# The head of an encoder kernel: x loaded by tokens, its squares summed along rows, and half of the bucket marks made on ScalarE

## The chip, the cores and the metric

One core of a Trainium2 chip runs the whole program in one launch. The time of a run is the device time of that core in microseconds (us). A profile of one execution stands beside the timed runs; its span goes from the first to the last instruction. The engines are named as in the profile: PE is TensorE (PEld its weight loads), DVE is VectorE, ACT is ScalarE, POOL is GpSimd, SP is SyncE, which here issues every load and store.

## What is computed

A trunk of two layers on one sequence of 256 tokens and 2048 features, in float32. Only what the head of the program touches matters here:

```python
cond = jax.nn.silu(c)
for l in range(DEPTH):
    mod = cond @ w_ada[l] + b_ada[l]
    sh_a, sc_a, g_a, sh_m, sc_m, g_m = jnp.split(mod, 6, axis=-1)
    h = _rmsnorm(x) * (1.0 + sc_a) + sh_a        # x / sqrt(mean(x*x) + eps), per token
    proj = h @ w_in[l]
    ...                                          # two kinds of attention, output projection
    # the first kind adds to its scores
    rel = positions[:, None, :] - pi[:, :, None]
    bias = bias_table[_t5_bucket(rel)]           # 32 buckets of relative distance
    ...
    x = x + g_a * mix
    ...                                          # adaLN again, squared-ReLU MLP of width 8192
return _rmsnorm(x, final_norm_g)
```

Of the 32 buckets, 16 are for keys ahead of the query and 16 for the others. In each half the buckets 0 to 7 hold a single distance each (0 to 7), the buckets 8 to 15 hold ranges of distances. One bucket, number 16 (ahead, at distance 0), never occurs.

## The kernel before

Activations are kept feature-major: `self.x` is 128 partitions (features of one k tile) by 16 k tiles by 256 tokens. Weights come from memory in f32; most are split into a rounded part and a rest (`weights`: `hi` made on ACT, `lo` on DVE) and go through PE in three products. The first six blocks of layer 0 are not split: `by_k` multiplies them whole (its line with `whole[k]`, L240).

Buffers come from pools that go round: five 8 KB buffers with tag `raw` for adaLN weights and unsplit weights, four each with tags `hi` and `lo` of 4 KB, six with tag `t` for short-lived activations, 40 with tag `u`, eight PSUM banks. A tile waits until the earlier holder of its buffer is done with. A scheduler writes the order of the instructions of each engine when the program is built; each engine then runs its own list strictly in order, and SP issues the loads in the order of its list.

The head runs in this order.

- `setup` loads `c`, the vectors, constants (`K`) and positions, and then x, already turned by the host (`xT`), as four loads of 512 KB. PE spreads `c` over all partitions (four products with a row of ones, `pc`), and ACT makes `cond` with Silu. `bias_setup` prepares positions and the bucket table on DVE and ACT.
- `sumsq` squares x on ACT, two k tiles at a time (eight squares of 128x512), and DVE adds the results up (seven adds). Then `rstd` lets PE sum over partitions (`pn`, four small products of 128x1 for the two token halves), ACT takes the square root, DVE the reciprocal, and PE spreads the result over the partitions with `ident`.
- `first_norm_then_by_k` takes the 16 k tiles in eight blocks p of two. For each block: DVE multiplies x by the norm (`ht`), four adaLN sums give the block's shift and scale (`ada_sums`: a pass of DVE over a 128x2048 weight tile against `cond`, twice for the shift and twice for the scale, and small adds that end in `mod`), ACT applies them (`hf`) and rounds (`h`), DVE makes the rest of the rounding, and PE multiplies by 24 weight tiles of `w_a` into six open PSUM banks.
- Into the first four blocks another piece is threaded (`FILL`): `bias_marks` and `bias_part` for a quarter of the bias table each. `bias_marks` makes eight marks, for four buckets each: ACT squares the distance to the bucket's centre (`sq`, 128x512), DVE compares it with the bucket's squared half width and writes ones and zeros (`oh`). `bias_part` multiplies the marks by the bucket table on PE (`pb`, 16 products), and ACT copies the result into `self.bias` at the next block.

The loads of a block are issued in this order: its four adaLN tiles (1 MB each), then its four weight tiles (384 KB each). An adaLN tile needs a free `raw` buffer, so its issue waits for the sum on DVE that has used up an older one, and the weight loads stand behind it in SP's list.

Of the kernel before, what the change touches and what calls it, by code (L numbers as in the profile page):

```python
# [9 lines left out]
F32 = mybir.dt.float32  # L10
F32R = mybir.dt.float32r
I32 = mybir.dt.int32
AF = mybir.ActivationFunctionType
ALU = mybir.AluOpType
AX = mybir.AxisListType

P = 128
T = 256
D = 2048
NK = D // P  # L20
# [22 lines left out]
C_W2 = 168  # L43
C_FREQ = 176
C_SGN = 177
NCONST = 178

V_BADA = 0
V_SUBLN = 192
# [20 lines left out]
def consts():  # L70
    c = np.zeros((P, NCONST), np.float32)
    p = np.arange(P)
    c[p, C_DELTA + p % 32] = 1.0
    c[p, C_PERM + (p ^ 32)] = 1.0
    for g in range(8):
        for r in range(4):
            b = 4 * g + r
            n = b % 16
            lo, hi = BUCKET_FROM[n], BUCKET_FROM[n + 1] - 1
            sign = -1.0 if b < 16 else 1.0  # L80
            rows = slice(32 * r, 32 * r + 32)
            if b == 16:
                c[rows, C_CB + g], c[rows, C_W2 + g] = 0.0, -1.0
            else:
                c[rows, C_CB + g] = -sign * (lo + hi) / 2.0
                c[rows, C_W2 + g] = ((hi - lo) / 2.0 + 0.25) ** 2
    c[:, C_FREQ] = np.asarray(INV_FREQ, np.float32)[p % 32]
    c[:, C_SGN] = np.where(p % 64 < 32, -1.0, 1.0)
    return c
# [10 lines left out]
class Trunk:  # L100
# [230 lines left out]
    def setup(self):  # L331
        nc, io, cp = self.nc, self.io, self.cp
        self.ada_plan()
        self.cond = cp.tile([P, D], F32, name="cond")
        row = self.wp.tile([1, D], F32, tag="raw", name="c_row", bufs=5)
        nc.sync.dma_start(row, io["c"])
        self.vec = cp.tile([P, NVEC], F32, name="vec")
        nc.sync.dma_start(self.vec, io["vec"])
        self.eps = cp.tile([P, 1], F32, name="eps")
        nc.gpsimd.memset(self.eps, EPS)  # L340
        self.K = cp.tile([P, NCONST], F32, name="K")
        nc.sync.dma_start(self.K, io["consts"])
        self.pos = cp.tile([P, T + 8], I32, name="pos")
        nc.sync.dma_start(self.pos, io["pos"])
        self.ones = cp.tile([P, P], F32, name="ones")
        nc.gpsimd.memset(self.ones, 1.0)
        self.bias_setup()
        self.rel = [self.bias_rel(0)]
        for j in range(4):
            c = slice(512 * j, 512 * j + 512)  # L350
            ps = self.bank("pc").rearrange("p a b -> p (a b)")
            nc.tensor.matmul(ps, self.ones[:1], row[:, c], start=True, stop=True)
            nc.scalar.activation(self.cond[:, c], ps, AF.Silu)
        self.ident = cp.tile([P, P], F32, name="ident")
        make_identity(nc, self.ident)
        self.x = cp.tile([P, NK, T], F32, name="x")
        for q in range(4):
            nc.sync.dma_start(self.x[:, 4 * q : 4 * q + 4], io["xT"][:, 4 * q : 4 * q + 4])
        acc = None
        for k in range(0, NK, 2):  # L360
            acc = self.sumsq(acc, self.x[:, k : k + 2])
        return acc

    def fills(self):
        m = {"l": self.lambdas, "r": self.rope_setup}
# [61 lines left out]
    def bias_marks(self, a):  # L427

        nc, K = self.nc, self.K
        half = lambda s, dt=F32: self.up.tile([P, 2 * T], dt, tag="u", name=self.name(s))  # L430
        r = self.rel.pop(0) if self.rel else self.bias_rel(a)
        self.marks = []
        for g in range(8):
            sq = self.t("sq")
            nc.scalar.activation(sq, r, AF.Square, bias=K[:, C_CB + g : C_CB + g + 1])
            oh = half("oh", F32R)
            nc.vector.tensor_scalar(oh, sq.rearrange("p a b -> p (a b)"), K[:, C_W2 + g : C_W2 + g + 1], None, ALU.is_le)
            self.marks.append(oh)

    def bias_part(self, a):  # L440
# [61 lines left out]
    def rstd(self, acc, n, warm=False):  # L502

        nc = self.nc
        bank = self.bank("pn")
        ps, r = bank[:, 0, :2], self.s("rms")
        acc = acc[:2] + acc[3:]
        if warm:
            self.warm(acc[-2], 8)
        for i, a in enumerate(acc):  # L510
            for t in range(2):
                nc.tensor.matmul(
                    ps[:, t : t + 1], a[:, t * P : (t + 1) * P], self.ones[:, :1],
                    start=i == 0 and t == 0, stop=i == len(acc) - 1 and t == 1, skip_group_check=True,
                )
        if warm:
            self.warm(acc[-1], 6)
        nc.scalar.activation(r, ps, AF.Sqrt, bias=self.eps, scale=1.0 / n)
        nc.vector.reciprocal(r, r)
        for t in range(2):  # L520
            nc.tensor.matmul(
                bank[:, 1, t * P : (t + 1) * P], r[:, t : t + 1].broadcast_to([P, P]), self.ident,
                start=True, stop=True, skip_group_check=True,
            )
        if warm:
            self.warm(acc[-1], 8)
        return bank[:, 1]

    def warm(self, a, n):

# [73 lines left out]
    def first_norm_then_by_k(self, acc, src, n, fill, early):  # L604


        ps, r = self.rstd(acc, D), self.tp.tile([P, T], F32, tag="t", name=self.name("rstd"))
        self.nc.scalar.activation(r, ps, AF.Copy)
        banks = self.open_banks(2 * n)
        h, whole, made = [], [], []  # L610
        sh, sc = self.mod[0, 0], self.mod[0, 1]

        def ready(p):
            k = 2 * p
            t = self.normed(r, k)
            for g in (0, 1):
                self.ada_need(0, g, k + 1)
            new, lows, ins = self.scaled(t, k, sh, sc, whole if p < WHOLE else None)
            h.extend(new)
            made.append(ins)  # L620
            return lows

        lows = ready(0)
        for p in range(8):
            blocks = self.by_k_weights([src[0, p, b] for b in range(2)], 2 * n, p < WHOLE)
            low = lows
            if p >= WHOLE:
                low()
            if fill:
                fill[0][0]()  # L630
            if p < 7:
                lows = ready(p + 1)
            self.by_k(banks, blocks, h, 2 * p, NK, 2 * n, whole if p < WHOLE else None)
            if p < WHOLE:
                low()
            if self.bias_out:
                self.bias_out(made[p])
                self.bias_out = None
            if fill:
                fill.pop(0)[1]()  # L640
            if p in early:
                early[p](h, whole)
        return h, banks
# [366 lines left out]
def _layout(i):  # L1010
    f = {k: np.asarray(v) for k, v in i.items()}
    a = {}
    a["xT"] = np.ascontiguousarray(f["x"][0].reshape(T, NK, P).transpose(2, 1, 0))
    a["c"] = np.ascontiguousarray(f["c"])
    pos = f["positions"][0]
    order = [j + 4 * t for j in range(4) for t in range(2)]
    posq = np.tile(pos.reshape(8, 32).T, (4, 1))[:, order]
    a["pos"] = np.ascontiguousarray(np.concatenate([np.broadcast_to(pos, (P, T)), posq], 1))
    a["consts"] = consts()
    feat = lambda v, n: v.reshape(n, P).T  # L1020
    vec = [feat(f["b_ada"][l], 96) for l in range(2)]
# [52 lines left out]
```

## Time and profile before

| | us |
|---|---|
| median of three runs | 2240.9 |
| lowest and highest of them | 2237.83, 2252.52 |
| the profiled execution, its own time | 2238.34 |
| its span | 2236.6 |
| PE busy | 2195.2 |
| DVE busy | 1665.8 |
| ACT busy | 1117.7 |

The profile's page lists the busy time of each engine, then the span in 40 slices of 56 us, where each digit is the busy share of a slice in tenths. Its other views, which are quoted below, are: the stretches (busy time of each engine in a window, with the clock granted to PE, the share of the DMA engines and their GB/s), the timeline (one row per instruction or per run of like ones: start, length, engine, line, operation, output and input; in brackets the idle time of the engine before it and what ended that), the groups of instructions by line and shape (count, busy time, mean of one in ns, idle time before and its cause), and the loads (size and the time from issue to landing). The length of a row is that of the whole run of instructions it stands for. Neighbouring instructions of one engine overlap a little in these records.

### The profile page before, as it was taken

To read this page: it belongs to the slowest core of one execution; us is meant where nothing else is said; L and a number is where in the kernel's file an instruction comes from. 1 tells how busy PE (TensorE), PEld (TensorE's weight loads), DVE (VectorE), ACT (ScalarE), POOL (GpSimd) and SP (SyncE) were. 2 spreads that over 40 slices of the span, in tenths; PEclk is the share of its full clock that TensorE was granted. 3 is DMA by queue.
4 is the path that set the end of the run, shared out by engine and by line. 5 is a ranking of instruction groups with operands and counts; after the bars stand their busy time and mean duration, and the time that the engine had idled before them with its cause. 6 is when DMAs were issued, how large, how long until landed. Compare 5 with 4: busy or idle time off the path is not lost.

```text
span 2236.6 us, 33121 instructions
## 1 busy us (share of the span) xinstructions
PE 2195.2 (98%) x13362; PEld 1957.4 (88%) x13362; DVE 1665.8 (74%) x2275; ACT 1117.7 (50%) x1657; POOL 1.9 (0%) x10
## 2 busy tenths in 40 slices
PE   6899999999999999999999999999999999999998
PEld 5799889998888888888899988989888888888887
DVE  7879879988878888887888776775665565565565
ACT  4445664455454355355445465544635534544553
POOL 0000000000000000000000000000000000000000
PEclk9999999999999999999999999999999999999999
DMA  9898778898888888888779666655555555555551
GB/s 387 308 380 305 271 275 315 315 349 317 322 319 308 313 313 317 310 305 315 297 265 350 248 245 224 238 210 191 200 189 188 189 188 189 188 188 188 189 188 76
DMA packets 85692, 585.53 MB, mean 262 GB/s; under 512 B 9505, under 2 KB 9889, under 8 KB 21409
## 3 DMA queue, kind: packets, MB, share of 16 engines
q1 hardware_dynamic: 85538, 583.42, 70.1%
q8 instruction: 104, 1.70, 0.3%
q14 instruction: 50, 0.41, 0.0%
HBM read 581.28 MB, written 2.10 MB: 261 GB/s over the span
## 4 chain that ended last, share of the span: by engine, by line
PE 92%; DVE 4%; ACT 1%; issue 1%; DVEq 0%; ACTq 0%
PE ps L196 42%; PE ps L197 21%; PE pk L177 4%; PE pk L176 4%; PE pk L178 4%; PE pk L240 3%; DVE ada L303 2%; PE pv L252 1%; PE pv L251 1%; PE pv L253 1%; DVE lo L141 1%; PE ps L176 1%; PE ps L177 1%; PE ps L178 1%; PE pw L533 1%
## 5 line engine op out<-in xcount | busy, mean ns | idle before, releaser
L141 DVE TENSOR_TENSOR lo<-raw,hi 128x1024 fp32r<-128x1024 f32 (+1 forms) x722 | 853.8, 1185 | 430.1 <-ACT hi L140 426.1
L140 ACT ACTIVATE hi<-raw 128x1024 fp32r<-128x1024 f32 (+1 forms) x722 | 740.2, 1028 | 824.2 <-PE ps L196 610.7
L196 PE MATMUL ps<-hid,hi 128*128 128x512 f32 x2048 | 718.0, 395 | 0.0
L196 PE MATMUL ps<-h,hi 128*128 128x512 f32 x1664 | 581.5, 394 | 0.0
L197 PE MATMUL ps<-hid,lo 128*128 128x256 f32 x2048 | 573.4, 280 | 0.0
L197 PE MATMUL ps<-h,lo 128*128 128x256 f32 x1664 | 465.7, 280 | 0.0
L196 PEld LDWEIGHTS ps<-hid,hi 128*128 128x128 f32 x2048 | 384.0, 188 | 91.6 <-DVE hid L170 1.3
L303 DVE SCALAR_TENSOR_TENSOR ada<-ada,cond 128x2048 f32<-128x2048 f32 x192 | 437.8, 2283 | 2.8 <-DMA ada<-in_w_ada 2.7
L197 PEld LDWEIGHTS ps<-hid,lo 128*128 128x128 f32 x2048 | 386.7, 189 | 0.1
L196 PEld LDWEIGHTS ps<-h,hi 128*128 128x128 f32 x1664 | 311.9, 187 | 72.6
L197 PEld LDWEIGHTS ps<-h,lo 128*128 128x128 f32 x1664 | 314.1, 189 | 0.0
L177 PE MATMUL pk<-h,hi 128*128 128x256 f32 x704 | 199.0, 283 | 0.0
L178 PE MATMUL pk<-h,lo 128*128 128x256 f32 x704 | 198.9, 283 | 0.0
L176 PE MATMUL pk<-h,hi 128*128 128x256 f32 x704 | 198.5, 284 | 0.0
L834 DVE SCALAR_TENSOR_TENSOR x<-ps,mod,x 128x256 f32<-128x256 f32 x272 | 131.2, 483 | 65.2 <-PE ps L197 60.5
L177 PEld LDWEIGHTS pk<-h,hi 128*128 128x128 f32 x704 | 135.1, 192 | 0.1
L178 PEld LDWEIGHTS pk<-h,lo 128*128 128x128 f32 x704 | 135.1, 192 | 0.0
L176 PEld LDWEIGHTS pk<-h,hi 128*128 128x128 f32 x704 | 134.6, 192 | 0.1
L240 PE MATMUL pk<-hf,w 128*128 128x256 f32 x384 | 90.0, 398 | 11.5 <-ACT hf L547 11.5
L240 PEld LDWEIGHTS pk<-hf,w 128*128 128x128 f32 x384 | 76.6, 201 | 24.0 <-ACT hf L547 12.7
L196 PE MATMUL ps<-mo,hi 128*128 128x512 f32 x192 | 69.0, 399 | 0.0
L196 PE MATMUL ps<-do,hi 128*128 128x512 f32 x192 | 68.9, 399 | 0.0
(205 smaller groups left out, 2283.8 us busy)
## 6 DMA issues: line engine op xcount, KB each, us to landing
raw<-in_w_m SPq DMA_DIRECT2D x232, 1024.0 KB, 4.9
ada<-in_w_ada SPq DMA_DIRECT2D x192, 1024.0 KB, 4.9
raw<-in_w_ob SPq DMA_DIRECT2D x24, 1024.0 KB, 5.1
raw<-in_w_m SPq DMA_DIRECT2D x32, 768.0 KB, 4.4
raw<-in_w_dv SPq DMA_DIRECT2D x16, 1024.0 KB, 4.8
raw<-in_w_a SPq DMA_DIRECT2D x20, 768.0 KB, 6.3
raw<-in_w_t SPq DMA_DIRECT2D x12, 1024.0 KB, 4.8
w<-in_w_a SPq DMA_DIRECT2D x24, 384.0 KB, 8.9
```

The lines of the kernel that those rows point to most:

```text
L140: nc.scalar.activation(hi, v, AF.Copy)
L141: ins = nc.vector.tensor_tensor(lo, v, hi.bitcast(F32), ALU.subtract)
L176: mm(ps, hi, x[0], start=first, stop=False, skip_group_check=shared)
L177: mm(ps, hi, x[1], start=False, stop=False, skip_group_check=shared)
L178: mm(ps, lo, x[0], start=False, stop=last, skip_group_check=shared)
L196: mm(ps.rearrange("p a b -> p (a b)"), hi, both, start=k == 0, stop=False)
L197: mm(ps[:, 0], lo, x, start=False, stop=k == nk - 1)
L240: self.nc.tensor.matmul(ps, v, whole[k], start=first, stop=last, skip_group_check=True)
L251: mm(ps, xh, hi, start=first and k == 0, stop=False)
L252: mm(ps, xh, lo, start=False, stop=False)
L303: ins = nc.vector.scalar_tensor_tensor(w, w, 1.0, self.cond, ALU.mult, ALU.mult, accum_out=acc[:, i : i + 1])
L834: self.nc.vector.scalar_tensor_tensor(x, ps[i][:, j], g[:, m + i : m + i + 1], x, ALU.mult, ALU.add)
```

## The change

The change has two parts, both in the head.

*x by tokens.* The host no longer turns x. Four loads of 512 KB bring it token-major into tiles `xt[t][h]` (128 tokens by 1024 features, t the token half, h the feature half), which use two buffers of tag `hi` and two of tag `lo`. ACT squares each of them with a sum along its row (`accum_out`), writing the squares themselves into the still unused `self.bias`. So a token's sum of squares is the sum of two numbers, which DVE adds. PE turns x with 32 transposes of 128x128, four to a PSUM bank, and ACT copies the eight banks to `self.x`. The square root, the reciprocal and the spreading over partitions are taken out of `rstd` into `spread` and are used as they were. `ident` is made earlier.

*Marks.* In each set of eight marks, the four that stand for buckets of a single distance (g = 0, 1, 4, 5) are made by ACT as relu(1 - sq), which is one where the squared distance is zero, and zero where it is one or more. Two constant columns give the bias of one (zero for the bucket that never occurs). The other four marks are still compares on DVE.

```diff
-NCONST = 178
+C_ONE = 178
+NCONST = 180
...
+    c[:, C_ONE : C_ONE + 2] = 1.0
+    c[:32, C_ONE + 1] = 0.0
...
+        self.ident = cp.tile([P, P], F32, name="ident")
+        make_identity(nc, self.ident)
+        xt = [[None, None], [None, None]]
+        for h in range(2):
+            for t in range(2):
+                xt[t][h] = self.wp.tile([P, D // 2], F32, tag=("hi", "lo")[h], name=self.name("xt"), bufs=4)
+                nc.sync.dma_start(xt[t][h], io["x"][t, :, D // 2 * h : D // 2 * h + D // 2])
         self.bias_setup()
...
-        self.ident = cp.tile([P, P], F32, name="ident")
-        make_identity(nc, self.ident)
         self.x = cp.tile([P, NK, T], F32, name="x")
-        for q in range(4):
-            nc.sync.dma_start(self.x[:, 4 * q : 4 * q + 4], io["xT"][:, 4 * q : 4 * q + 4])
-        acc = None
-        for k in range(0, NK, 2):
-            acc = self.sumsq(acc, self.x[:, k : k + 2])
-        return acc
+        tot = self.sp.tile([P, 2, 2], F32, tag="s22", name="xsq")
+        for h in range(2):
+            for t in range(2):
+                junk = self.bias[:, 2 * t : 2 * t + 2].rearrange("p a b c -> p (a b c)")
+                nc.scalar.activation(junk, xt[t][h], AF.Square, accum_out=tot[:, h, t : t + 1])
+        for h in range(2):
+            for p in range(4):
+                ps = self.bank("px")
+                for i in range(2):
+                    c = (2 * p + i) * P
+                    for t in range(2):
+                        nc.tensor.transpose(ps[:, i, t * P : (t + 1) * P], xt[t][h][:, c : c + P], self.ident)
+                k = 8 * h + 2 * p
+                nc.scalar.activation(self.x[:, k : k + 2], ps, AF.Copy)
+        return tot
...
-            nc.vector.tensor_scalar(oh, sq.rearrange("p a b -> p (a b)"), K[:, C_W2 + g : C_W2 + g + 1], None, ALU.is_le)
+            if g % 4 < 2:
+                c = C_ONE + (g == 4)
+                nc.scalar.activation(oh, sq.rearrange("p a b -> p (a b)"), AF.Relu, bias=K[:, c : c + 1], scale=-1.0)
+            else:
+                nc.vector.tensor_scalar(oh, sq.rearrange("p a b -> p (a b)"), K[:, C_W2 + g : C_W2 + g + 1], None, ALU.is_le)
...
+    def spread(self, out, r, tot, n):
+
+        nc = self.nc
+        nc.scalar.activation(r, tot, AF.Sqrt, bias=self.eps, scale=1.0 / n)
         nc.vector.reciprocal(r, r)
         for t in range(2):
             nc.tensor.matmul(
-                bank[:, 1, t * P : (t + 1) * P], r[:, t : t + 1].broadcast_to([P, P]), self.ident,
+                out[:, t * P : (t + 1) * P], r[:, t : t + 1].broadcast_to([P, P]), self.ident,
                 start=True, stop=True, skip_group_check=True,
             )
...
-        ps, r = self.rstd(acc, D), self.tp.tile([P, T], F32, tag="t", name=self.name("rstd"))
+        ps, r, s = self.bank("pn")[:, 1], self.tp.tile([P, T], F32, tag="t", name=self.name("rstd")), self.s("rms")
+        self.nc.vector.tensor_tensor(s, acc[:, 0], acc[:, 1], ALU.add)
+        self.spread(ps, s, s, D)
         self.nc.scalar.activation(r, ps, AF.Copy)
...
-    a["xT"] = np.ascontiguousarray(f["x"][0].reshape(T, NK, P).transpose(2, 1, 0))
+    a["x"] = np.ascontiguousarray(f["x"][0].reshape(2, P, D))
```

The scheduler writes new lists for the head. In the changed program's lists ACT does the four row squares, the eight copies and then the square root; DVE has the reciprocal between the second and the third adaLN sum; and in a set of marks ACT alternates pairs of squares and pairs of Relus while DVE does an adaLN sum before its first and another between its second and third compare. From the fifth block on the lists of the two programs are the same.

More of the change, by code (lines that the diff above doesn't have):

```diff
@@ L517, in rstd @@
             self.warm(acc[-1], 6)
-        nc.scalar.activation(r, ps, AF.Sqrt, bias=self.eps, scale=1.0 / n)
+        self.spread(bank[:, 1], r, ps, n)
+        if warm:
+            self.warm(acc[-1], 8)
+        return bank[:, 1]
+    def spread(self, out, r, tot, n):
+        nc = self.nc
+        nc.scalar.activation(r, tot, AF.Sqrt, bias=self.eps, scale=1.0 / n)
         nc.vector.reciprocal(r, r)
@@ L521, in rstd @@
             nc.tensor.matmul(
-                bank[:, 1, t * P : (t + 1) * P], r[:, t : t + 1].broadcast_to([P, P]), self.ident,
+                out[:, t * P : (t + 1) * P], r[:, t : t + 1].broadcast_to([P, P]), self.ident,
                 start=True, stop=True, skip_group_check=True,
             )
-        if warm:
-            self.warm(acc[-1], 8)
-        return bank[:, 1]
     def warm(self, a, n):
```

## The prediction

> **What bounds the kernel now.** I read the page first, for what bounds the whole, then the stretches of the head, then the head in order of time.
>
> ```profile
> span 2236.6 us, 33121 instructions
> PE 2195.2 (98%) x13362; PEld 1957.4 (88%) x13362; DVE 1665.8 (74%) x2275; ACT 1117.7 (50%) x1657; POOL 1.9 (0%) x10
> PE   6899999999999999999999999999999999999998
> ```
>
> TensorE (PE) is busy for 2195.2 of 2236.6 us, so some 41 us in all are without it, and the slices show where: the first ones. The change edits only the head, so nothing it does can be worth more than a part of those 41 us, unless it makes PE wait anew. The stretches (PE, weight load, VectorE, ScalarE, GpSimd; then clock, DMA share, GB/s) say what limits the head.
>
> ```profile
> 42.00:56.00 14.00, 14.00 (x66) 12.12 (x65) 11.36 (x20) 8.97 (x16) 0.00 (x0) 1.00 1.02 415
> 84.00:98.00 14.00, 12.44 (x55) 10.33 (x53) 13.65 (x20) 4.94 (x9) 0.53 (x1) 0.97 0.78 298
> 98.00:112.00 14.00, 13.13 (x54) 11.38 (x55) 13.62 (x28) 6.17 (x11) 0.00 (x0) 0.88 0.78 276
> 112.00:126.00 14.00, 14.00 (x67) 12.32 (x66) 9.76 (x11) 1.70 (x4) 0.00 (x0) 1.00 0.96 375
> ```
>
> Until 98 us VectorE (DVE) is the fullest engine; the DMA queues are full until 56 us, then have a fifth to spare. From 98.87 us PE no longer waits (row below). So the question is by how much the change brings forward the start of the fifth block of matmuls, at 98.87. What ran before:
>
> ```profile
> 2.63 7.16 PE L352 MATMUL pc<-c_row,ones 1*128 1x512 f32 x8 [2.63 <-DMA c_row<-in_c]
> 6.76 0.56 SPq L287 DMA_DIRECT2D ada<-in_w_ada  x1
> 8.62 0.62 ACT L498 ACTIVATE sqx<-x 128x512 f32<-128x512 f32 x1
> 11.36 2.69 ACT L498 ACTIVATE sqx<-x 128x512 f32<-128x512 f32 x5
> 14.57 2.28 DVE L303 SCALAR_TENSOR_TENSOR ada<-ada,cond 128x2048 f32<-128x2048 f32 x1
> 20.38 0.69 DVE L499 TENSOR_TENSOR acc<-acc,sqx 128x512 f32<-128x512 f32 x1
> 21.13 1.86 PE L512 MATMUL pn<-ones,acc 128*128 128x1 f32 x8 [11.34 <-DVE acc L499]
> 23.07 1.28 ACT L518 ACT_TABLE_LOAD   x1 [9.02 <-PE pn L512]
> 23.69 2.09 SPq L221 DMA_DIRECT2D w<-in_w_a  x4
> 24.66 0.17 DVE L519 RECIPROCAL rms<-rms 128x2 f32<-128x2 f32 x1 [1.38 <-ACT rms L518]
> 27.55 0.15 DVE L313 SCALAR_TENSOR_TENSOR mod<-macc,vec 128x2 f32<-128x2 f32 x1
> 28.40 13.18 PE L240 MATMUL pk<-hf,w 128*128 128x256 f32 x48 [2.23 <-ACT hf L547]
> 43.29 0.16 DVE L313 SCALAR_TENSOR_TENSOR mod<-macc,vec 128x2 f32<-128x2 f32 x1
> ```
>
> ScalarE (ACT) has squared x by 14.05, but the adds of the squares share DVE with the adaLN sums (L303), and the last add starts only at 20.38. PE's sum over features, the table load and the square root follow, and the reciprocal comes at 24.66. Block p (a pair of k tiles) can begin when its `mod` is done: block 0 at 27.55, block 1 at 43.29.
>
> Then a loop, here from block 2 to block 3:
>
> ```profile
> 61.46 0.16 DVE L313 SCALAR_TENSOR_TENSOR mod<-macc,vec 128x2 f32<-128x2 f32 x1
> 61.66 1.09 ACT L547 ACTIVATE hf<-ht,mod,mod 128x256 f32<-128x256 f32 x2 [9.10 <-DVE mod L313]
> 63.09 0.43 DVE L555 TENSOR_TENSOR h<-hf,h 128x256 fp32r<-128x256 f32 x1 [0.68 <-ACT h L549]
> 63.39 1.79 ACT L451 ACTIVATE bias<-pb 32x512 f32<-32x512 f32 x3
> 63.77 0.42 DVE L555 TENSOR_TENSOR h<-hf,h 128x256 fp32r<-128x256 f32 x1
> 65.20 5.01 ACT L435 ACTIVATE sq<-rel,K 128x512 f32<-128x512 f32 x8
> 65.96 1.72 DVE L437 TENSOR_SCALAR oh<-sq,K 128x512 fp32r<-128x512 f32 x3 [1.77 <-ACT sq L435]
> 67.59 2.29 DVE L303 SCALAR_TENSOR_TENSOR ada<-ada,cond 128x2048 f32<-128x2048 f32 x1
> 69.80 2.07 DVE L437 TENSOR_SCALAR oh<-sq,K 128x512 fp32r<-128x512 f32 x5
> 71.78 0.69 DVE L537 TENSOR_TENSOR ht<-x,rstd 128x512 f32<-128x512 f32 x1
> 79.61 0.15 DVE L313 SCALAR_TENSOR_TENSOR mod<-macc,vec 128x2 f32<-128x2 f32 x1
> 98.87 36.27 PE L240 MATMUL pk<-hf,w 128*128 128x256 f32 x160 [2.43 <-ACT hf L547]
> ```
>
> From `mod` to `mod` 18.15 us (61.46 to 79.61). DVE works through it but for two waits on ACT: 0.7 for `h` and 1.77 for the first squared distance, since ACT does `hf`, `h` and three bias copies first. PE waits: of the 14 us of 84 to 98 it has 1.6 free.
>
> **The change part by part.** Prices, from the groups (line, engine, shapes; busy, mean ns):
>
> ```profile
> L437 DVE TENSOR_SCALAR oh<-sq,K 128x512 fp32r<-128x512 f32 x32 | 14.3, 482 | 6.6 <-ACT sq L435 5.7
> L435 ACT ACTIVATE sq<-rel,K 128x512 f32<-128x512 f32 x32 | 20.1, 708 | 0.1
> L140 ACT ACTIVATE hi<-raw 128x1024 fp32r<-128x1024 f32 x618 | 653.0, 1058 | 709.7 <-PE ps L196 599.2 <-PE pv L253 29.3 <-PE pk L177 26.1
> L884 ACT ACTIVATION_READ_ACCUMULATOR sm<-sm,mxm 128x1 f32 x32 | 6.1, 192 | 0.0
> L270 ACT ACTIVATE aT<-pt 128x512 f32<-128x512 f32 x24 | 14.2, 591 | 2.4 <-PE pt L915 2.4
> 24.98 1.19 PE L521 MATMUL pn<-ident,rms 128*128 128x128 f32 x4 [1.98 <-DVE rms L519]
> ada<-in_w_ada SPq DMA_DIRECT2D x1, 1024.0 KB, 14.9
> ```
>
> Neighbours on one engine overlap by about 0.1: five squares of 0.62 in 2.69 stand 0.52 apart, eight of 0.71 in 5.01 stand 0.61 apart.
>
> *The head on ACT.* Removed: eight squares, seven DVE adds, PE's eight small sums. Added: four row squares of 128x1024 with a read of the accumulator, 32 transposes on PE, eight copies of 128x512 from PSUM. No row has the row square; nearest is the 1024 wide conversion with its 1.058, plus 0.192 for the accumulator: 1.25 apart at most, 1.05 with overlaps, which I take. In between still stand one conversion (`lsch`) and one `cond`, both 512 wide, 0.52 each. In ACT's order of the changed program the copies come ahead of the square root. So from 8.62, when the first square runs now: 4 x 1.05 + 2 x 0.52 + 8 x 0.49 = 9.2, the last copy done at 17.8; from table load to reciprocal it takes 1.6 (23.07 to 24.66), so the reciprocal comes at 19.4. Unoverlapped prices give 21.2.
>
> The transposes could hold the copies up. PE starts on them when its four `cond` products end, at 9.8 (2.63 + 7.16). The four 128-wide records at L521 took 1.19, 0.30 each: 32 at that rate end at 19.4, the last copy at 20.0, the reciprocal comes at 21.6. L521 has two matmuls in four records, an f32 product being done in two passes; a transpose passes once and I take half: PE ends at 14.6, before ACT asks for its last bank.
>
> On DVE the order of the changed program is sum 1, a 128x2 add, sum 2, reciprocal, sum 3, `ht`, sum 4, `mod`. The reciprocal waits for the root, and sums 3 and 4 are queued behind it, with the loads that take their buffers. A sum takes 2.28, 2.21 apart; sum 1 begins at 14.57 as now, so sum 2 ends at 19.0 and the wait is short. Then 19.4 + 0.1 + 2.21 + 0.60 (`ht`) + 2.21 + 0.08 = 24.6 for `mod`, against 27.55: **3.0 us** earlier. The bound: the fourth adaLN tile, issued at 6.76, lands 14.9 later, at 21.7, so `mod` is not before 24.0, a gain of 3.6 at most; a reciprocal at 21.6 leaves 0.8.
>
> *Loads.* Four x loads of the same size stand at the same place of SP's queue. They borrow half of the `hi`/`lo` buffers, so block 1's weights now wait for transposes and squares too, which are over by 20 us even at the upper price, while those loads are issued at 23.69 in any case. That costs nothing; past 23.7 each microsecond would hold back every adaLN load queued behind them on SP.
>
> *Marks.* In each of four mark sets, four of eight compares leave DVE (0.41 apart, 1.65 us) and become a Relu on ACT with a bias operand. No row has it; L435 is the same shape with the same kind of operand: 0.61 apart, 0.52 without that operand as a floor, 0.71 without overlap as a ceiling. One loop round by the changed order, from `mod`: ACT reaches the squares at +3.74 as now; two squares, two Relus, then the third square, done at 3.74 + 4 x 0.61 + 0.71 = +6.9. DVE has meanwhile finished `rel` and the lows (+2.65) and one adaLN sum, pulled ahead (+4.9), and waits 2.0. Two compares (to +7.9), a sum (+10.1), a compare; the last compare needs the eighth square, behind four more squares and two more Relus, at +11.2, a wait of 0.7. Then +11.6, `ht` +12.2, sum, two `rt`, sum, `mod`: +17.4. So the saved 1.65 shrinks to **0.75 a round**, for ACT's longer order is a new wait in the place of the work removed. Three rounds (blocks 1 to 4): 2.2 us, 1.2 to 3.5 between floor and ceiling. From block 0 to block 1 (15.74 now, 43.29 - 27.55) the same count gives 15.2: **0.5**, 0.1 to 1.0 with the same bounds.
>
> *Sum.* 3.0 + 0.5 + 2.2 = 5.7 us at the fifth block. After it both programs have the same instructions in the same order on every engine, PE is the bound, and each load is released by work that moves along. So 2238.3 (the profiled execution: span 2236.6 and 1.7 around it) becomes 2232.6. The median of the runs shown, 2240.9, lies 2.6 above that execution, their lowest at 2237.8; I put half of the offset on: **2234**. Bounds of the terms: 0.8 + 0.1 + 1.2 to 3.6 + 1.0 + 3.5, or 2.1 to 8.1 us.
>
> PE's clock adds something the order does not fix. It shows 0.88 in 98 to 112: the 160 matmuls take 36.27, 0.227 each.
>
> ```profile
> 143.77 6.91 PE pk L240 x32
> ```
>
> At 0.216 each they would take 34.6, so the slow spell costs 1.7 on the path, behind a gap of 2.43 us in PE. The changed kernel keeps a gap there, since its `mod` still comes after PE has run dry, so I keep the spell in the sum.
>
> **The rivals.**
> *The transfers set the pace.* DMA share is 1.02 in 42 to 56 and 0.96 behind 112; if data come no earlier, an earlier `mod` buys nothing: 2238.3, in the runs up to 2241. For it: these shares. Against it: the fourth tile lands 2.9 before the new `mod`, and 0.78 in 84 to 112 is free room.
> *Slower: ScalarE becomes the loop's bound.* The place is the compare that waits for the eighth square. A Relu dearer by d makes a round longer by 4d; with the four sets the gain of 5.7 is gone at 16d, that is at a Relu of 0.97 us. At 1.06, as for the 1024 wide conversion, it costs 1.5 us net: 2239.8; at 1.25, 2242.8. For it: ACT already sets DVE's 1.77 wait. Against it: no 512 wide row of ACT shown here costs over 0.71.
> [...]
> *The head does not do what it says.* The root waits behind the copies, and with the ceilings for squares and transposes the norm gains 0.8 only: 3.5 in all, 2234.8 in the profile, 2236 in the runs. For it: the row square is the one operation without a row of its own. Against it: its parts have rows.
> *The slow spell goes.* A fifth block that starts with PE at full clock wins 1.7 more: 2230.9, in the runs 2232. Against it: a gap of 2.43 was enough for the spell. [...]
>
> **How the numbers follow.** Forecast 0.56, late norm 0.14, slow spell gone 0.10, transfers 0.11, slower loop 0.09. The range reaches from 2228 (bounds of the gain at 8, and the slow spell gone) to 2242 (no gain, with the offset of the runs). One per cent, 22 us, is about what a measurement of this kernel can tell from no change; none of these cases reaches it, since a gain that size would need half of PE's 41 us without work. I leave 0.02 for faster, 0.04 for slower by something that I do not see, and 0.94 within.
>
> **What would show it.** Right: the reciprocal near 19.4, the first matmul of block 0 (now L243) near 25.4, rounds of 17.4 with two waits of DVE on ACT, the 160-matmul run starting near 93.2, and the same length from there to the end. Wrong: the reciprocal behind 22 (norm), rounds of 18 and more with DVE waiting for `sq` (loop), DVE waiting for `ada` from DMA (transfers), or a longer stretch after the fifth block, which would upset the claim that the rest only moves.

## The result, and the profile after

| | us | |
|---|---|---|
| before, median of 20 runs | 2239.14 | 2233.45 to 2252.52 |
| changed, median of 20 runs | 2233.74 | 2227.09 to 2246.41 |
| ratio changed to before | 0.9973 | 95% interval 0.9961 to 0.9984 |
| changed, the profiled execution | 2236.08 | span 2234.2 (before 2236.6) |

The kernel is faster by 0.27%, 6.0 us by the ratio (3.6 to 8.7). That is a gain that 20 runs resolve and that lies well within one per cent.

The head of the changed kernel, from its timelines (start, length, engine, line, operation, output and input, count; in brackets the idle time of the engine and what ended it):

```profile
9.68 5.94 PE L376 MATMUL px<-ident,xt 128*128 128x128 f32 x32
12.69 1.05 ACT L369 ACTIVATE bias<-xt 128x1024 f32<-128x1024 f32 x1
13.64 0.19 ACT L369 ACTIVATION_READ_ACCUMULATOR bias<-xt 128x1 f32 x1
13.73 3.99 ACT L378 ACTIVATE x<-px 128x512 f32<-128x512 f32 x8
17.74 1.28 ACT L547 ACT_TABLE_LOAD   x1
19.42 0.16 DVE L548 RECIPROCAL rms<-rms 128x2 f32<-128x2 f32 x1
24.62 0.16 DVE L316 SCALAR_TENSOR_TENSOR mod<-macc,vec 128x2 f32<-128x2 f32 x1
25.47 13.52 PE L243 MATMUL pk<-hf,w 128*128 128x256 f32 x48 [4.61 <-ACT hf L573]
```

The last row square begins at 12.69 and the copies follow without a gap, so PE's transposes hold nothing up. `mod` of block 0 comes at 24.62 instead of 27.55. The four `mod` behind it, and the fifth block of matmuls:

```profile
39.80 0.16 DVE L316 SCALAR_TENSOR_TENSOR mod<-macc,vec 128x2 f32<-128x2 f32 x1
58.01 0.16 DVE L316 SCALAR_TENSOR_TENSOR mod<-macc,vec 128x2 f32<-128x2 f32 x1
76.76 0.15 DVE L316 SCALAR_TENSOR_TENSOR mod<-macc,vec 128x2 f32<-128x2 f32 x1
94.28 0.15 DVE L316 SCALAR_TENSOR_TENSOR mod<-macc,vec 128x2 f32<-128x2 f32 x1
95.12 36.49 PE L243 MATMUL pk<-hf,w 128*128 128x256 f32 x160 [3.23 <-ACT hf L573]
```

Rounds of 15.18, 18.21, 18.75 and 17.52, where before they were 15.74, 18.17, 18.15 and 18.42. Only the first and the last are shorter. The fifth block starts at 95.12, 3.75 earlier than before and 1.9 later than the 93.2 of the prediction. What made the two rounds in the middle long:

```profile
42.70 1.79 ACT L472 ACTIVATE bias<-pb 32x512 f32<-32x512 f32 x3 [0.99 <-PE pb L469]
47.58 1.10 DVE L458 TENSOR_SCALAR oh<-sq,K 128x512 fp32r<-128x512 f32 x2 [2.84 <-ACT sq L452]
64.95 1.10 DVE L458 TENSOR_SCALAR oh<-sq,K 128x512 fp32r<-128x512 f32 x2 [2.01 <-ACT sq L452]
69.24 0.49 DVE L458 TENSOR_SCALAR oh<-sq,K 128x512 fp32r<-128x512 f32 x1 [0.58 <-ACT sq L452]
74.89 0.17 ACT L394 ACTIVATE lam_e<-pl 128x4 f32<-128x4 f32 x1 [5.06 <-PE pl L393]
...
76.61 0.23 DVE L400 SCALAR_TENSOR_TENSOR lam<-lam_e 128x1 f32<-128x1 f32 x2 [1.26 <-ACT lam_e L395]
```

The waits that come in every round are those of 64.95 and 69.24: 2.01 and 0.58. In the round before, ACT's bias copies wait 0.99 for PE's `pb`, the squares queued behind them come late, and DVE waits 2.84. In the round after, DVE waits 1.26 for `lam_e`: ACT makes it from `pl`, which PE multiplies behind all `pb` products, and `lam` stands ahead of `mod` on DVE.

Whether the gain arrives: the first update of x behind the attention, in the view of the tile `mod` (duration least, median, most; first and last start), before and then after:

```profile
L828 DVE SCALAR_TENSOR_TENSOR x<-pk,mod,x x8: 474/474/483, 351.8 to 1430.7; 128x256 f32<-128x256 f32 x8
```

```profile
L856 DVE SCALAR_TENSOR_TENSOR x<-pk,mod,x x8: 474/476/484, 348.1 to 1427.5; 128x256 f32<-128x256 f32 x8
```

That is 3.7 us at 350, as at the fifth block, and 3.2 at 1430.

### The profile page after: what moved, and what is told of

The parts are those of the page before. It is cut to its first block, busy times and chain, and to the rows that moved or that the text cites. A ratio compares the mean times of both kernels' runs of the same rounds, so it can differ in the third digit from the quotient of the medians.

```text
span 2234.2 us, 33164 instructions
## 1 busy us (share of the span) xinstructions
PE 2200.3 (98%) x13386; PEld 1963.3 (88%) x13386; DVE 1654.8 (74%) x2253; ACT 1131.5 (51%) x1681; POOL 1.9 (0%) x10
## 4 chain that ended last, share of the span: by engine, by line
PE 93%; DVE 4%; ACT 2%; DMA 1%; issue 1%; SPq 0%; DVEq 0%; ACTq 0%
PE ps L199 41%; PE ps L200 21%; PE pk L180 4%; PE pk L181 4%; PE pk L179 4%; PE pk L243 3%; DVE ada L306 2%; PE pv L255 1%; PE pv L254 1%; PE pv L256 1%; DVE lo L144 1%; PE ps L179 1%; PE ps L180 1%; PE ps L181 1%; PE pw L559 1%; PE po L956 1%
## 5 line engine op out<-in xcount | busy, mean ns | idle before, releaser
L243 PE MATMUL pk<-hf,w 128*128 128x256 f32 x384 | 90.4, 399 | 12.8 <-ACT hf L573 12.8
```

What stands on the lines that cost most here:

```text
L243: self.nc.tensor.matmul(ps, v, whole[k], start=first, stop=last, skip_group_check=True)
```

## The experiments

One execution differs from the next, so each kernel is read at three places: the start of the fifth block, the first update of x (as in the rows above), and the ratio over the runs.

| kernel | rounds from `mod` to `mod` | fifth block | first update of x | ratio (95%) |
|---|---|---|---|---|
| before | 15.74, 18.17, 18.15, 18.42 | 98.87 | 351.8 | 1 |
| changed | 15.18, 18.21, 18.75, 17.52 | 95.12 | 348.1 | 0.9973 (0.9961 to 0.9984) |
| e1 head alone | 15.52, 17.99, 18.14, 18.65 | 95.71 | 350.5 | 0.9990 (0.9967 to 1.0013) |
| e2 marks alone | 15.81, 17.11, 17.39, 17.53 | 96.22 | 347.5 | 0.9975 (0.9953 to 0.9997) |
| e3 PE kept awake | 15.19, 17.10, 17.83, 17.52 | 94.11 | 345.4 | 0.9971 (0.9949 to 0.9993) |
| e4 lambdas later | 15.18, 17.30, 17.39, 17.54 | 92.77 | 344.1 | 0.9964 (0.9939 to 0.9990) |
| e5 bias copies behind marks | 15.18, 16.06, 16.06, 16.22 | 89.45 | 341.8 | 0.9951 (0.9932 to 0.9970) |
| e6 compares first | 13.46, 15.60, 15.58, 17.07 | 86.99 | 340.1 | 0.9945 (0.9926 to 0.9964) |
| e7 Relus twice | 17.02, 17.41, 17.63, 19.92 | 97.48 | 350.0 | 0.9987 (0.9971 to 1.0002) |
| e8 changed, once more | 15.19, 18.06, 17.40, 17.52 | 93.59 | 345.9 | one run |
| e9 ten unread matmuls | 13.67, 15.59, 15.58, 17.09 | 89.60 | 342.0 | 0.9942 (0.9923 to 0.9962) |
| e10 lambdas in block 5 | 13.45, 15.59, 15.58, 17.05 | 86.93 | 339.0 | 0.9940 (0.9925 to 0.9954) |

The theory (A) is this: the count of the rounds was right, and what it left out is PE at half clock (a granted clock of 0.50 in the stretches; a half-clock spell is such a time). Its lateness reaches DVE through ACT's queue, by the bias copies and by `lam_e`. The rival (B): these waits belong to the new order on ACT and DVE, whatever PE's clock does.

**e1, the head alone.** The Relu branch is taken out again:

```diff
-            if g % 4 < 2:
-                ... activation(oh, sq, AF.Relu, ...)
-            else:
-                nc.vector.tensor_scalar(oh, ...)
+            nc.vector.tensor_scalar(oh, ...)
```

> The changed head without the marks on ScalarE: all eight compares of a set stay on VectorE. By the sum of the prediction the head is worth about 3 us and nothing is given back after it: mod of block 0 at 24.6 (27.55 before), rounds of 15.7, 18.15, 18.15 and 18.4 as before the change, the fifth block's matmuls near 95.9 (98.87 before), the run some 3 us shorter, a ratio of 0.9987. The rival: the head's gain is not kept, since TensorE wakes no earlier and its later bias matmuls hold ScalarE up in the rounds behind; then the fifth block starts at 97 or later and the ratio is 0.9993 or more.

Measured: `mod` of block 0 at 24.56, rounds within 0.25 of those before the change, the fifth block 3.16 earlier. The head's term is there in full. In this execution the 48 matmuls of block 2 took 12.31, as long as those of block 3 in the kernel before, whose clock is 0.50 from 81.39 to 84.80, and DVE waited 0.41 for `lam_e` even with the old marks. At the first update of x only 1.3 is left. The first 55 matmuls of the fifth block took 14.54, some 2.6 more than at the 0.2175 each of e10 below, where the 160 of the kernel before took 1.5 more; that is 1.1 of the 1.9 that are missing, and I did not follow the rest. The ratio is too wide to say more.

**e2, the marks alone.** The kernel before, with the Relu branch and its two constant columns.

> The old head (x read feature-major, squares summed by VectorE), with the four marks of a set on ScalarE. By the prediction: mod of block 0 at 27.55, a first round of 15.2, then 17.4 three times, the fifth block's matmuls near 96.2, a ratio of 0.9988. By what the changed kernel's trace shows, two of the three rounds behind pay a wait that was not there before, ScalarE's bias copies for the pb matmuls and VectorE's lam for lam_e: then rounds of 15.2, 18.2, 17.5 to 18.7 and 17.5, the fifth block near 97 to 98, a ratio of 0.9992 to 0.9997. Which of the two waits shows depends on where TensorE's half-clock spell falls.

Its timeline at the `mod` of blocks 2 and 3, with the lambda between them:

```profile
60.47 0.16 DVE L316 SCALAR_TENSOR_TENSOR mod<-macc,vec 128x2 f32<-128x2 f32 x1
77.72 0.22 DVE L386 SCALAR_TENSOR_TENSOR lam<-lam_e 128x1 f32<-128x1 f32 x2
77.86 0.15 DVE L316 SCALAR_TENSOR_TENSOR mod<-macc,vec 128x2 f32<-128x2 f32 x1
```

Rounds of 17.11, 17.39 and 17.53: the 17.4 of the prediction, and `lam` waits for nothing. The orders on ACT and DVE are those of the changed kernel in these rounds, so rival B is in trouble: what differs is PE, whose blocks 1, 2 and 3 took 10.52, 10.63 and 10.63 here, where block 2 of the changed kernel took 12.20. The first round, 15.81, missed the 15.2: with the old head DVE waits 1.38 for the first `sq` there. Marks alone 2.65 and head alone 3.16 make 5.8 at the fifth block, as the sum of the prediction has it (5.7); both together made 3.75.

**e3, PE kept awake.** Unread matmuls in the gaps:

```diff
+WARM = {0: 14, 2: 16, 4: 20}
...
+            if p in WARM:
+                self.warm(r, WARM[p])
             self.by_k(banks, blocks, h, 2 * p, ...)
```

> The changed kernel with matmuls that nothing reads put into TensorE's gaps ahead of block 0 (14), block 2 (16) and block 4 (20); the instructions of the other engines keep their order. Theory A (the two lost rounds are TensorE's half clock, which arrives at VectorE through ScalarE's bias copies and through lam_e): block 0 runs at full clock from about 25 and takes 10.6 instead of 13.5, the 0.99 wait of the bias copies and the 1.26 wait of lam are both under 0.3, rounds near 15.2, 17.5, 17.5, 17.5, the fifth block's matmuls at 93.2 as the prediction had it and without a half-clock spell there (another 1.7): the fifth block ends 3.6 us earlier than in the changed kernel, ratio to the kernel before about 0.9957. Theory B (the waits come from the order on ScalarE and VectorE, whatever TensorE does): rounds as in the changed kernel, 15.2, 18.2, 18.7, 17.5, at most the 1.7 of the fifth block is won, ratio 0.9965.

Block 0 takes 10.53, the wait of the bias copies is gone, that of `lam` is 0.34, blocks 1, 2 and 3 take 10.52, 10.53 and 10.63, and the granted clock is 1.00 from 89.60 to 112.00: theory A on the waits. The start of the fifth block is a miss, by my own sizing, as two rows of PE show (the second is cut off by the end of the view):

```profile
89.65 4.63 PE L560 MATMUL pw<-rstd,ident 128*128 128x128 f32 x40
94.11 3.19 PE L244 MATMUL pk<-hf,w 128*128 128x256 f32 x14
```

Twenty matmuls (two records each) take 4.46 us, and the block, whose `mod` starts at 92.20, starts behind them at 94.11, 1.1 later than at its usual 0.83 behind `mod`. The 16 ahead of block 2 were too many as well (54.90 to 58.47, `mod` at 56.85): that block started 0.8 late, and the round behind it, with the 0.34 of `lam`, is 17.83.

**e4, the lambdas later.**

```diff
-FILL = "0|1|2|l3|r"
+FILL = "0|1|2|3|rl"
```

> The changed kernel with the lambdas' small work one fill later, behind the rotary angles, so that on VectorE lam stands behind mod of block 4 and no longer ahead of mod of block 3. If lam's wait for lam_e is what made the round from block 2 to block 3 long, that round is 17.5 instead of 18.75, the fifth block's matmuls start 1.2 us earlier, near 93.9, and the ratio to the kernel before is about 0.9968. If the wait only moves (VectorE then waits as long for something else TensorE sets, such as the squares behind the bias copies), the round stays above 18.3 and the ratio at 0.9973.

The round from block 2 to block 3 is 17.39, and the fifth block comes at 92.77, better than expected. But in this execution block 2 also took 10.63 and not 12.20, so the row does not separate the place of `lam` from the clock; e8 does.

**e8, the changed kernel once more.** Nothing is changed.

> The changed kernel, profiled once more. [...] Theory B (the waits belong to this kernel's order): 18.2 and 18.75 again, to 0.1.

Its timeline, and then its stretches ahead of blocks 2 and 3 and at the start of each (PE, weight load, DVE, ACT and GpSimd busy; clock, DMA share, GB/s):

```profile
57.83 0.16 DVE L316 SCALAR_TENSOR_TENSOR mod<-macc,vec 128x2 f32<-128x2 f32 x1
58.68 10.63 PE L243 MATMUL pk<-hf,w 128*128 128x256 f32 x48 [2.21 <-ACT hf L573]
75.09 0.22 DVE L400 SCALAR_TENSOR_TENSOR lam<-lam_e 128x1 f32<-128x1 f32 x2
75.23 0.15 DVE L316 SCALAR_TENSOR_TENSOR mod<-macc,vec 128x2 f32<-128x2 f32 x1
76.07 13.66 PE L243 MATMUL pk<-hf,w 128*128 128x256 f32 x48 [2.97 <-ACT hf L573]
```

```profile
54.92:58.33 3.41, 1.55 (x7) 0.94 (x5) 3.38 (x9) 0.30 (x1) 0.00 (x0) 1.00 1.01 425
58.33:61.75 3.42, 3.07 (x14) 2.74 (x15) 2.74 (x6) 3.35 (x8) 0.00 (x0) 1.00 0.99 418
72.00:75.42 3.42, 1.10 (x7) 0.85 (x5) 3.42 (x10) 1.67 (x4) 0.00 (x0) 1.00 0.76 266
75.42:78.83 3.41, 2.76 (x7) 2.20 (x8) 2.74 (x6) 3.36 (x7) 0.00 (x0) 0.50 1.00 395
```

The same in the first profile of the changed kernel:

```profile
55.26:58.67 3.41, 1.41 (x7) 0.83 (x5) 3.38 (x7) 0.46 (x1) 0.00 (x0) 1.00 1.01 428
58.67:62.08 3.41, 3.22 (x8) 2.59 (x9) 2.74 (x5) 3.34 (x8) 0.00 (x0) 0.50 0.99 413
75.74:79.15 3.41, 1.55 (x7) 1.40 (x8) 1.87 (x8) 3.01 (x7) 0.00 (x0) 1.00 1.00 405
79.15:82.57 3.42, 3.42 (x18) 3.01 (x17) 2.53 (x3) 3.37 (x7) 0.00 (x0) 1.00 1.05 432
```

This decides for A against B on the second wait, for which B had a round of 18.75 again. The program is the same. In the first profile the clock fell ahead of block 2, its 48 matmuls took 12.20, and `lam` waited 1.26; here block 2 ran at full clock in 10.63, `lam` waited for nothing, and the round is 17.40. The spell came one block later, where DVE did not wait for PE: its round is 17.52 in spite of 13.66 us of matmuls. The round from block 1 to block 2 is 18.06, with 0.84 of wait in the bias copies; block 0 again took long, 13.39. For this first wait e8 alone does not decide, but e3 and e4, whose lists on ACT and DVE are those of the changed kernel in this round, do: where block 0 took 13.52, 13.39, 12.63 (e4) and 10.53 (e3), the copies waited 0.99, 0.84, and twice under 0.1, and the round was 18.21, 18.06, 17.30 and 17.10. The first 76 matmuls of the fifth block took 16.67, 0.219 each (0.228 for the 160 of the first profile), and x is 5.9 earlier than before the change.

**e7, each Relu twice.**

```diff
-                nc.scalar.activation(oh, sq, AF.Relu, ...)
+                for _ in range(2):
+                    nc.scalar.activation(oh, sq, AF.Relu, ...)
```

> The changed kernel with each of its 16 Relus issued twice into the same tile, which makes a Relu dearer by 0.61. The rival of the prediction (ScalarE bounds the loop, a round longer by 4d) gives 2.4 us a round in the order of the changed kernel, 9.8 in all, the fifth block near 104 and a ratio of 1.0015. In this kernel's order VectorE has an adaLN sum more ahead of the last two compares, so that by a count it waits some 3.2 and 0.6 for sq, and rounds are near 18.5: then the fifth block starts at 97 to 99 and the ratio is 0.9985 to 1.0000, and the price of 4d belongs to one order and not to the change.

The fifth block starts at 97.48, still 1.4 ahead of the kernel before; the ratio is 0.9987, with an interval that reaches just past one. DVE waits longer for `sq` but once a round:

```profile
67.25 0.49 DVE L459 TENSOR_SCALAR oh<-sq,K 128x512 fp32r<-128x512 f32 x1 [3.23 <-ACT sq L452]
78.98 0.23 DVE L400 SCALAR_TENSOR_TENSOR lam<-lam_e 128x1 f32<-128x1 f32 x2 [2.10 <-ACT lam_e L395]
```

In this execution blocks 2 and 3 took 13.52 and 12.29, against 12.20 and 10.63 in the first profile of the changed kernel. Sixteen Relus more cost 2.4 us against the first profile of the changed kernel and 3.9 against the second, not 9.8. The scheduler put an adaLN sum in front of the late compares. So the rival's price, and with it its break-even at 0.97 us, did not hold: they were worked out for a frozen order. What dearer Relus cost in the changed kernel's own order is not shown, since no run keeps it.

**e5, the bias copies behind the marks.** On top of e4, ACT's copies are ordered behind the last square of the next set instead of behind `h`:

```diff
...
-                self.bias_out(made[p])
+                self.bias_out(self.last or made[p])    # last: the eighth square of the set
```

> The kernel of the later lambdas, in which besides ScalarE's copies of the finished bias come behind the next set's squares and marks instead of three of them ahead. VectorE's order does not change. If VectorE's 2.0 wait for sq is the three copies (1.79) and nothing else, squares start as soon as rel is clipped: first square done at mod + 2.9, the third at + 5.4, VectorE's wait before the first compares falls from 2.0 to some 0.5 and the second stays at 0.3 to 0.6: rounds of 15.9 to 16.1 instead of 17.4, the fifth block's matmuls at 88.5 to 89 (92.8 in the run of the later lambdas), ratio to the kernel before 0.994 to 0.9945. The rival (transfers set the pace): the loads of a round need at least 15.8 us at the rate of 25 to 45, so VectorE waits for ada from DMA instead, and the rounds stay at 16.5 or more.

Rounds of 16.06, as counted; the fifth block comes at 89.45, a little late, since `lam_e` now delays its `hf`. ACT's squares now wait for DVE's `rel`, and not DVE for ACT's copies:

```profile
58.28 1.34 ACT L452 ACTIVATE sq<-rel,K 128x512 f32<-128x512 f32 x2 [0.52 <-DVE rel L441]
61.49 1.10 DVE L460 TENSOR_SCALAR oh<-sq,K 128x512 fp32r<-128x512 f32 x2 [0.70 <-ACT sq L452]
```

The 2.01 has become 0.70. So the wait that the prediction foresaw was for the most part, 1.3 of 2.0, the three copies.

**e6, the compares first.** On top of e5:

```diff
-        for g in range(8):
+        for i, g in enumerate((2, 3, 6, 7, 0, 1, 4, 5)):
...
```

> The kernel with the bias copies behind the marks, in which besides the four marks that VectorE compares are made ahead of the four Relus in each set. VectorE then finds its squares in a row, 0.61 apart, and by a count in the new order a round is 15.4 from mod to mod with no second wait on ScalarE. If no other resource limits, the fifth block's matmuls start near 87 and the ratio is 0.9935. If the transfers set the pace below 15.8 to 16 us a round, VectorE shows waits for ada from DMA and the fifth block starts near 88.5 to 89, no better than without this edit.

Two rounds of 15.60 and 15.58, with one wait for `sq` of 0.46 for all four compares, and no wait for data:

```profile
45.00:85.00 40.00, 39.00 (x179) 33.33 (x177) 36.77 (x57) 28.72 (x51) 0.53 (x1) 1.00 1.02 424
56.69 2.33 DVE L460 TENSOR_SCALAR oh<-sq,K 128x512 fp32r<-128x512 f32 x4 [0.46 <-ACT sq L452]
```

The DMA share is 1.02 through the whole stretch, and DVE still finds its tiles there, so the transfers do not set the pace at 15.6 us a round, and the 15.8 that e5 gave as the least for a round's loads is no floor. The fifth block is near the 87 that was expected, though not by four like rounds: the first, 13.46, is 1.7 shorter than in e5, and the last is 17.07 since the scheduler put a second `ht` and work on the rotary angles ahead of its `mod`. The 160 matmuls of the fifth block took 36.49, as in the first profile of the changed kernel.

**e9 and e10, ten unread matmuls ahead of the fifth block.** On top of e6; e10 also moves the lambdas:

```diff
+WARM = {4: 10}
...
-FILL = "0|1|2|3|rl"          # e9
+FILL = "0|1|2|3|r|l"         # e10
```

> The kernel with the compares first, and ten matmuls that nothing reads in TensorE's gap ahead of the fifth block (2.65 us there; the 20 of the earlier run took 4.46 us, 0.223 each, and held the fifth block up by 1.07, so ten take 2.2). If the spell at the fifth block follows the gap, it does not show, the fifth block starts near 87 and runs at full clock from its start, 1.7 us won: ratio to the kernel before about 0.9938. If the spell comes in spite of it, or the ten are late and hold the block up, it is as without them, 0.9945.

In e9 the spell is gone (the first 95 matmuls of the fifth block take 20.77, 0.219 each), but the block starts at 89.60, 3.0 behind its `mod`. The scheduler had put `pl` behind the ten, and on ACT `lam_e` ahead of `hf`:

```profile
87.36 0.17 ACT L395 ACTIVATE lam_e<-pl 128x4 f32<-128x4 f32 x1 [5.56 <-PE pl L394]
87.55 1.28 ACT L396 ACT_TABLE_LOAD   x1
...
88.96 1.08 ACT L576 ACTIVATE hf<-ht,mod,mod 128x256 f32<-128x256 f32 x2
```

> As the run before (compares first, bias copies behind the marks, ten unread matmuls ahead of the fifth block), but with the lambdas' work two fills further on, in block 5's, so that neither pl nor ScalarE's table load for the exponential stands between mod and hf of the fifth block. In the run before, lam_e came at 87.36 behind the ten matmuls and the fifth block started at 89.60, 3.0 after its mod; now it starts 0.8 after mod, near 87.2, with TensorE at full clock: 2.4 us better than the run before and 1.7 better than the kernel with the compares first, ratio to the kernel before about 0.9935. If the fifth block comes no earlier, something else than the table load held hf.

In e10 they are out of the way:

```profile
84.00 2.39 PE L562 MATMUL pw<-rstd,ident 128*128 128x128 f32 x20
86.93 34.80 PE L244 MATMUL pk<-hf,w 128*128 128x256 f32 x160 [0.54 <-ACT hf L576]
```

The fifth block starts 0.83 behind `mod` and its 160 matmuls take 34.80 instead of 36.49: the 1.7 us that the prediction priced a spell at. The 0.54 of idle time that is left ahead of it is less than the 2.20 ahead of the changed kernel's block 2, which took 12.20; in e9 2.27 is left, and there is no spell either. In e10 x is 12.8 earlier than before the change, 1.1 better than e6 and not 1.7; where the other 0.6 stayed I did not follow. The ratio of 0.9940 lies wholly below that of the changed kernel (0.9954 against 0.9961 at the nearest): e10 beats both kernels. The ratios of e5, e6, e9 and e10 lie within each other's intervals, so their order rests on the profiles alone.

## Why the prediction was right, and where it was not

*The head, 3.0 us.* Right, step by step: reciprocal 19.42 (19.4), `mod` 24.62 (24.6), first matmul 25.47 (25.4). The row square without a row of its own took 1.05 and 0.19, spaced 1.04 to 1.09, as its parts had said. The transposes took 0.186 each, somewhat over the half of 0.30, ended at 15.6, and still were ahead of ACT.

*Block 0 to block 1, 0.5 us.* Right: 15.18, a gain of 0.56.

*Three rounds of 17.4, 2.2 us.* The count was right and the term was not. The Relu is 0.61 from the next instruction, the two waits are 2.01 and 0.58 for the forecast 2.0 and 0.7, and rounds of 17.39 to 17.54 stand in e2, e4 and e8. In the profiled execution, though, the three rounds together took 54.48 where they had taken 54.74: 0.3 instead of 2.2. In the second execution it was 1.8, with 52.98. The step that failed is the claim that the loop is DVE's alone, with PE's clock a matter of the fifth block only. One of its own rows spoke against it: DVE is not the fullest engine in every stretch until 98 us, for from 42 to 56 PE is busy for 14.00 of 14.00 and DVE for 11.36. PE is behind there, since its block 0 took 13.18 where block 1 took 10.52. A round shortened on DVE uses up the slack of what PE delivers: `pb` for ACT's copies, and `pl` for `lam_e`. Of that last slack the trace of before had a row that I had not read, on ACT between `lam_e` and the next `hf`:

```profile
78.25 0.21 ACT L378 ACTIVATE lam_e<-lam_e 128x4 f32<-128x4 f32 x1
79.80 1.09 ACT L547 ACTIVATE hf<-ht,mod,mod 128x256 f32<-128x256 f32 x2 [1.34 <-DVE mod L313]
```

`lam_e` was done at 78.46, 1.15 before `mod`. By the sum block 2, and `lam_e` with it, comes 4.25 earlier and this `mod` 5.0, which leaves 0.4. That is enough with PE at full clock. With the spell block 2 took 12.20 instead of 10.63, so `lam_e` is 1.2 too late, about the 1.26 measured.

*The slow spell, kept at the fifth block.* It was there in the profiled execution, but the reason given, that a gap of this length brings one, is too simple. In the second execution the fifth block had none, and elsewhere too gaps of like length went both ways (the gaps and times stand in the last section). What decides is not shown.

*Loads at no cost, and transfers as a rival.* Right but for one row. In the rounds of the changed kernel DVE waits for data once: the adaLN sum that starts at 28.26, in the round from block 0 to block 1, waits 0.46 for its tile. It cost that round nothing: in e4 DVE has no such wait, waits 0.83 instead of 0.28 for the next `sq`, and the round is 15.18 as well. From block 1 on there is none, and e6 runs at 15.6 a round.

*ScalarE as a bound.* That d on a Relu costs 4d a round did not come true in e7, where the scheduler wrote another order.

*Then the rest only moves.* The gain of the fifth block is that at 350 us. From there on the two programs' instructions are the same in the same order (DVE's lists differ at one place before that, an `ht` one adaLN sum earlier, at 99.75 instead of 106.50). Yet the gain does not stay. Two stretches before and after, PE busy for all but some 0.2 us, at full clock:

```profile
400.00:800.00 400.00, 399.77 (x2500) 359.07 (x2499) 342.36 (x438) 196.78 (x273) 0.00 (x0) 1.00 0.85 318
800.00:1200.00 400.00, 400.00 (x2421) 354.91 (x2420) 339.49 (x430) 197.08 (x265) 0.53 (x1) 1.00 0.81 305
```

```profile
400.00:800.00 400.00, 399.79 (x2478) 357.87 (x2479) 339.81 (x432) 195.22 (x271) 0.00 (x0) 1.00 0.85 316
800.00:1200.00 400.00, 400.00 (x2448) 357.80 (x2447) 341.90 (x435) 197.91 (x266) 0.53 (x1) 1.00 0.83 308
```

The changed kernel did 22 matmuls fewer in the first and 27 more in the second. The same `mod` near 700, before and after, shows the whole gain gone:

```profile
697.64 0.15 DVE L315 TENSOR_TENSOR mod<-macc,vec 128x2 f32<-128x2 f32 x1
```

```profile
697.66 0.15 DVE L318 TENSOR_TENSOR mod<-macc,vec 128x2 f32<-128x2 f32 x1
```

By 1100 us 3.1 of it is back. This is not the change's doing, for the changed kernel's second execution goes another way: against the kernel before it is 5.8 ahead at 400, 0.4 behind at 900, 2.6 ahead at 1400 and 0.7 behind at 2200. So the end of a single profile does not price the head.

*The number.* 2238.3 less 5.7, with half of the offset on, gave 2234; the median is 2233.7. Over 20 runs the kernel before has its median only 0.8 above its profile, so little of the offset was real. That the number came out within 0.3 is in part luck: in the two profiled executions the fifth block gained 3.75 and 5.28, not 5.7, and the offset of 1.3 went on top. The gain of 6.0 by the runs (3.6 to 8.7) holds the 5.7 and the 3.75 alike, so the runs do not tell the right count from the short one; the rounds do.

## What to carry to other kernels

When an edit shortens a loop that one engine sets, list for that engine and for each one it waits on what else stands in their in-order queues, and compare the slack of each delivery with the time you win: here, in the first profile, three small copies and a 128x1 `lam` took the gain of two rounds out of three. Put work that nobody waits for behind the work that somebody does (the bias copies behind the marks were worth 1.3 us a round). A single profile cannot price a term that depends on where PE runs at half clock, which was at block 2 in one profile of the changed kernel and at block 3 in the other: profile the same program twice before a wait is blamed on its order.

## What the hardware showed that I had not expected

*Like gaps, with a spell and without one.* Four spells at the blocks stand in the profiles of the two kernels, from 81.39 to 84.80 and from 98.46 to 101.87 before the change, from 58.67 to 62.08 and from 96.21 to 99.62 after it. The blocks in them began behind 3.72, 2.43, 2.20 and 3.23 of idle PE. But with 2.21 (block 2 in e8), 2.75 (block 3 after the change), 2.99 (block 3 in e2) and 3.09 (block 2 before the change, block 3 in e4) the 48 matmuls took 10.63, against the 12.20 behind 2.20. So the length of the gap alone does not tell in these runs. In the stretches shown with e8, PE is busy for 1.41 and 1.10 us of 3.41 ahead of the two spells, and for 1.55 in the two that no spell followed; that is four rows, and I make no rule of them.

*The clock rose while PE turned x.* Stretches of the changed kernel's head:

```profile
9.70:14.29 4.59, 4.59 (x23) 4.59 (x23) 1.91 (x4) 4.59 (x11) 0.00 (x0) 1.00 1.02 419
14.29:17.71 3.42, 1.33 (x12) 1.10 (x10) 3.03 (x4) 3.42 (x8) 0.00 (x0) 1.00 1.00 422
```

The clock's first record is at 14.29; the column shows 1.00 ahead of it for want of one. Transposes start 0.213 apart until then and 0.109 apart behind. The kernel before has the same `pc` products until 9.79 and no transposes behind them, and its first clock record is at 33.60; 12 matmuls stand in the 5.60 us ahead of that (28.00 to 33.60), 17 in the 3.41 behind (33.60 to 37.01). In the changed kernel the full clock was lost again at 17.71, behind the second stretch, of which PE fills 1.33, and the clock is 0.50 until 31.36, so block 0 began at half clock.

*Matmuls at full clock are not all equally fast.* In the kernel before, matmuls with outputs of 128x512 (`ps`, L196) alternate with smaller ones. From 750 to 800 us the next matmul starts 230 ns behind each of the 144, and from 900 to 950 it starts 233, 236 and 241 ns behind them in turn, at a granted clock of 1.00 in both. Such a rhythm holds for stretches of a hundred us and more and then changes: the kernel before has the even one from 750 to 850 and the uneven one from 900 to 1050, the changed kernel the uneven one from 550 to 700 and the even one from 750 to 1050. Its cause stays open; it may be a part of why single runs of one kernel lie up to 19 us apart.
